# One decoder layer on one core: weights loaded in pairs, joined rows, a gate table laid out by tile

## The chip, the cores and the metric

One Trainium2 chip; the kernel runs on one of its cores. TensorE (PE in the profile) multiplies matrices, VectorE (DVE), ScalarE (ACT) and GpSimd (POOL) do elementwise work, SyncE (SP) issues transfers. The metric is device time in microseconds (us), lower is better.

## The reference

512 tokens of 1024 features go through one layer: a layer norm, two token mixers (a gated linear recurrence and pooled means), a second layer norm, and a mixer that looks up experts. This last part matters here. Each token picks 128 of 16384 experts (8 heads, 16 each) by its queries, with a gate for each:

```python
def peer_ffn(x, w_query, sub_keys, u_tab, v_tab):
    ...                                   # top 16 of each half, then of their sums
    expert = i1 * PEER_NKEYS + i2
    gate = jax.nn.softmax(best_v, axis=-1).astype(x.dtype)
    ...
        u = u_tab[et]
        act = jax.nn.gelu(jnp.einsum('td,tkd->tk', xt, u), approximate=False) * gt
        return jnp.einsum('tk,tkd->td', act, v_tab[et])
    ...
h = layer_norm(ALPHA * h + ffn + ple, ln2_g[l], ln2_b[l])
```

## The kernel before

The program has three stretches. In stage A (0 to about 445 us) PE works through the projections and the token mixers. In stage B (to about 924 us) the experts of all tokens are chosen. In stage C (to the end) the expert values are summed.

The experts are handled in two ways. The first 128 tokens (NG = 1 block) fetch the table rows they picked: an indirect transfer, issued by POOL in `issue`, brings one row of `u_tab` for each token (128x1024, 512 KB), and `consume` lets DVE multiply it with the token and sum (L984, the dot). After 128 of those one Gelu is taken of all the dots, and 128 rows of `v_tab` follow, which DVE adds with their gate (L987, the add). Two fetched rows share one buffer of 8 KB for each partition, of which there are four (`big`, pool `vt`); the layer norm's gain and bias (`gb`, from `gain_bias`) keep one of them from the start of stage C.

The other 384 tokens (ND) go over all 16384 experts densely, in NT = 128 tiles of 128 experts. For a tile `key_product` multiplies a tile of `u_tab` (128x1024) with the tokens on PE (24 matmuls `fp`), ACT takes the Gelu (`ge`, L633), `weigh` lets DVE multiply by the gates of this tile (`ge<-ge,gt`, L1009), `split_act` splits the product into two parts (ACT writes `ah`, DVE `al`; both L118/L119), and `values` multiplies them with a tile of `v_tab` and sums over all tiles in PSUM (18 matmuls `yacc`). Every matmul is done as three (L123 to L125) of split operands. So a weight tile (`wraw`) is also split, by `fetch`: ACT writes `wh` (L219) and DVE `wl` (L220), up to two tiles ahead of their use. The three `wraw` buffers hold 512 KB each.

The products of 52 tiles (NS) are made in stage B already and kept in DRAM (`Hs`), from where SP loads them back (`ge<-Hs`). `order` is the order of the tiles in stage C: eight tiles, and then stored and unstored ones in alternation. I call an iteration of the loop over tiles a U iteration if it also makes a key product, for the tile LEAD = 6 places later (70 of the 128), and a V iteration if not (58).

The gates of the dense tokens are built in stage B: PE makes them for 16 tokens at a time (`pG`), ACT copies them to `stg`, and SP writes 1 MB (`Gd<-stg`) to a DRAM table `Gd`, 24 times. In stage C `g_load` brings the gates for eight tiles at once (`gt<-Gd`, 1.5 MB, 16 times). In `Gd` the gates of 16 tokens and all experts stand together, so that such a load takes 24 pieces of 512 bytes for each partition. It is issued with the tile seven places ahead (`key_load`); three buffers hold gate tiles, and one more (`g0p`) the first.

The order of instructions on each engine in stages B and C is the order of the program text (`manual_schedule`), so each queue is in order: whatever waits holds all behind it on its engine. SP's queue holds nearly all loads. An iteration i of the loop before:

```python
key_load(i + LEAD + 1)
split_act(i + 1)
key_product(i + LEAD)
vals[i] = take()            # fetch: loads and splits weight tiles ahead
...                         # values(i, b), then consume() and issue()
weigh(i + LEAD)
```

Of the kernel before, what the change touches and what calls it, by code (L numbers as in the profile page):

```python
# [18 lines left out]
D = 1024  # L19
# [26 lines left out]
GEB = 9  # L46
W0 = ((1, 2), (3,), (), ())
PACE = (4, (1,))


@with_exitstack
def hybrid_block(ctx, tc, ins, out, dbg=None):
# [85 lines left out]

    def load_w(src):
        t = wp.tile([128, 1024], FT, name="wraw", tag="wraw", bufs=3)  # L140
        nc.sync.dma_start(t, src)
        return t
# [36 lines left out]
    order = list(range(NS, NS + VG))  # L179
    later = NT - NS - VG  # L180
    for i in range(NS + later):
        nf = (i + 1) * later // (NS + later)
        order.append(NS + VG + nf - 1 if nf > i * later // (NS + later) else i - nf)

    def u_src(e):
        return ins["u_tab_t"][e]

    def v_src(e):
        return ins["v_tab"][e * 128:(e + 1) * 128, :]

    act_hi, dve_hi, pool_lo, dve_lo = nc.scalar.copy, nc.vector.tensor_copy, nc.gpsimd.tensor_sub, nc.vector.tensor_sub
    stream, nu = [], 0
    for i in range(2 * H):
        stream.append((ins["w_query"][i], act_hi, pool_lo))
        for _ in range(UQ[i]):
            stream.append((u_src(nu), act_hi, pool_lo))
            nu += 1
    for q in range(4):
        stream += [(ins["w_ple_gate"][q, k], act_hi, pool_lo) for k in range(2)]
        for _ in range(UP[q]):  # L200
            stream.append((u_src(nu), act_hi, pool_lo))
            nu += 1
    stream += [(u_src(e), act_hi, dve_lo) for e in range(nu, NS)]
    for i in range(-LEAD, NT):
        if i + LEAD < NT and order[i + LEAD] >= NS:
            stream.append((u_src(order[i + LEAD]), act_hi, dve_lo))
        if i >= 0:
            stream.append((v_src(order[i]), act_hi, dve_lo))
    raws, parts, pos_ = {}, {}, [0, 0, 0]

    def fetch(n):
        while pos_[1] < min(n + 6, len(stream)) or pos_[2] < min(n + 3, len(stream)):
            if pos_[2] < min(n + 3, len(stream)) and pos_[1] - pos_[2] >= min(3, len(stream) - pos_[2]):
                i = pos_[2]
                _, f, g = stream[i]
# [3 lines left out]
                f(hi, raw)  # L219
                g(lo, raw, hi.bitcast(FT))  # L220
                parts[i] = (hi, lo)
                pos_[2] += 1
            else:
                raws[pos_[1]] = load_w(stream[pos_[1]][0])
                pos_[1] += 1
# [10 lines left out]
    with ExitStack() as pa:  # L236
        t2 = pa.enter_context(tc.tile_pool(name="t2", bufs=15))
# [235 lines left out]
        def att2(h):  # L473
            x = hd[h]
            v, hs = head(h)
            st = hp.tile([128, NB, DK], FT, name="st", bufs=2)
# [146 lines left out]
    Gd = dram.tile([ND // TG, 128, 128 * TG], FT, name="Gd")  # L623
# [41 lines left out]
    g0p = ctx.enter_context(tc.tile_pool(name="g0p", bufs=1))  # L665
# [10 lines left out]
    with ExitStack() as pb:  # L676
        rt = pb.enter_context(tc.tile_pool(name="rt", bufs=1))
        eqp = pb.enter_context(tc.tile_pool(name="eqp", bufs=3))
# [220 lines left out]
        def evacuate(s, p):  # L899
# [4 lines left out]
            if t4 == TG // 4 - 1:  # L904
                nc.sync.dma_start(Gd[g], stgs.pop(g).rearrange("p i t -> p (i t)"))
# [43 lines left out]
        g_load(order[0], g0p)  # L949
# [4 lines left out]
    with ExitStack() as pc:  # L954
# [5 lines left out]
        todo = [(0, b, k) for b in range(NG) for k in range(128)] + [(1, b, k) for b in range(NG) for k in range(128)]  # L960
        half_n = len(todo) // 2
        got, cnt, pair = {}, [0, 0], [None]

        def issue():
# [3 lines left out]
            kind, b, k = todo[n]  # L968
            if n % 2 == 0:
                pair[0] = big("rows").rearrange("p (a b) c -> p a (b c)", a=2)  # L970
            r = pair[0][:, n % 2, :]
            got[n] = r
            nc.gpsimd.indirect_dma_start(out=r, out_offset=None, in_=ins["v_tab" if kind else "u_tab"],  # L973
                                         in_offset=bass.IndirectOffsetOnAxis(ap=eidx[:, b, k:k + 1], axis=0))
            cnt[0] += 1

        def consume():
            n = cnt[1]
            if n >= len(todo) or n not in got:
                return  # L980
            kind, b, k = todo[n]
            r = got.pop(n)
            if kind == 0:
                nc.vector.scalar_tensor_tensor(r, r, 1.0, hg[:, b, :], op0=OP.mult, op1=OP.mult,  # L984
                                               accum_out=hdot[:, b, k:k + 1])
            else:
                nc.vector.scalar_tensor_tensor(hres[:, b, :], r, ggate[:, b, k:k + 1], hres[:, b, :],  # L987
                                               op0=OP.mult, op1=OP.add)
            cnt[1] += 1

        def key_load(i):
            if i < NT:
                g_load(order[i], gp)
# [22 lines left out]
        g2, b2 = gain_bias(2)  # L1016
# [34 lines left out]

        for i in range(LEAD + 1):
            key_load(i)
        for i in range(LEAD):
            key_product(i)
            weigh(i)
        split_act(0)
        GL = 4
        for _ in range(GL):
            issue()  # L1060
        share, tot = 0.0, sum(2 if e >= NS else 1 for e in order[:NT - TAIL - EARLY])
        budget = 0.0
        wait_n = 0
# [93 lines left out]
```

## Time and profile before

| | us |
|---|---|
| median of three runs | 1796.36 (1795.77 to 1797.86) |
| the profiled execution | 1800.53 |
| its span in the trace | 1798.8 |

The span is that of the trace's instructions; 1.7 us of the profiled execution lie around it. That execution is 4.2 us (0.23%) over the median. PE is busy in 97% of the span, DVE in 74%, ACT in 42%, POOL in 36%. An engine's busy time counts neither its waiting nor the issuing of transfers. "Wait" rows say which engine stood idle, ahead of which operation, and what ended it.

### The profile page before, as it was taken

The numbers are of one execution on the slowest core, as the hardware profiler recorded it, in microseconds if no ns is written. First come the engines' busy times: TensorE is split into PE (matmuls) and PEld (weight loads), VectorE is DVE, ScalarE is ACT, GpSimd is POOL, SyncE is SP. The second block draws the span as 40 slices with busy tenths as digits, with TensorE's granted clock in tenths as the row PEclk, the third lists the DMA queues.
The fourth block names the chain that finished last, engine by engine and source line by source line (L and its number), as shares of the span: only waits on it lengthen the run. The fifth ranks groups of instructions, "written<-read, shape, count | busy, mean of one in ns | idle before, by whom it ended". The sixth has DMA issues, their size and how long they took to land.

```text
span 1798.8 us, 25265 instructions
## 1 busy us (share of the span) xinstructions
PE 1750.0 (97%) x9677; PEld 1537.9 (85%) x9677; DVE 1327.0 (74%) x2332; ACT 749.4 (42%) x1052; POOL 644.5 (36%) x421
## 2 busy tenths in 40 slices
PE   7999999999999999999989999999999999999997
PEld 5888887888888998898989888888888888888886
DVE  6367764155589689999847797877867888878787
ACT  3578862332322445565643333333333333333332
POOL 3533333443355520000013453453433444445440
PEclk9999999999999999999999999999999999999999
DMA  4322222431333345565698999899998999899983
GB/s 147 117 83 71 71 74 93 127 123 60 108 105 107 97 138 183 192 229 202 236 303 291 350 344 366 314 331 331 315 331 295 338 352 343 301 342 338 320 303 104
DMA packets 159694, 399.10 MB, mean 222 GB/s; under 512 B 12882, under 2 KB 75858, under 8 KB 156372
## 3 DMA queue, kind: packets, MB, share of 16 engines
q1 hardware_dynamic: 115220, 253.02, 42.1%
q0 software_dynamic: 36864, 134.23, 20.9%
q10 hardware_dynamic: 7488, 10.23, 1.6%
q8 instruction: 76, 1.25, 0.3%
q14 instruction: 46, 0.38, 0.1%
HBM read 359.94 MB, written 37.49 MB: 221 GB/s over the span
## 4 chain that ended last, share of the span: by engine, by line
PE 82%; DVE 8%; DMA 6%; issue 2%; ACT 1%; SPq 0%; POOL 0%; ACTq 0%; DVEq 0%; POOLq 0%
PE fp L123 15%; PE fp L125 15%; PE fp L124 15%; PE yacc L124 8%; PE yacc L125 8%; PE yacc L123 8%; DMA wraw<-in_v_tab_dram 3%; PE ple L847 3%; PE pG L896 2%; DVE A L882 2%; DVE wl L220 2%; PE acc L124 1%; PE acc L125 1%; PE acc L123 1%; DVE oh L876 1%
## 5 line engine op out<-in xcount | busy, mean ns | idle before, releaser
L123 PE MATMUL fp<-othi,wh 128*128 128x384 f32 (+1 forms) x1216 | 430.1, 354 | 0.3 <-ACT othi L136 0.3
L125 PE MATMUL fp<-othi,wl 128*128 128x384 f32 (+1 forms) x1216 | 420.8, 346 | 5.5 <-DVE wl L220 5.5
L220 DVE TENSOR_TENSOR wl<-wraw,wh 128x1024 fp32r<-128x1024 f32 x246 | 300.9, 1226 | 163.1 <-ACT wh L219 161.3
L124 PE MATMUL fp<-otlo,wh 128*128 128x384 f32 (+1 forms) x1216 | 420.0, 345 | 0.2 <-DVE otlo L137 0.2
L219 ACT CAST wh<-wraw 128x1024 fp32r<-128x1024 f32 x280 | 294.3, 1053 | 300.5 <-DMA wraw<-in_v_tab_dram 192.6
L973 POOL DMA_INDIRECT rows<-in_u_tab_dram,eidx x128 | 178.6, 1395 | 499.7 <-DVE oh L876 249.3
L123 PE MATMUL yacc<-wh,ah 128*128 128x512 f32 x768 | 300.9, 392 | 6.2 <-ACT wh L219 6.2
L124 PE MATMUL yacc<-wl,ah 128*128 128x512 f32 x768 | 302.6, 394 | 3.6 <-DVE wl L220 3.6
L125 PE MATMUL yacc<-wh,al 128*128 128x512 f32 x768 | 301.9, 393 | 0.0
L973 POOL DMA_INDIRECT rows<-in_v_tab_dram,eidx x128 | 188.3, 1471 | 224.0 <-DVE hres L987 188.5
L119 POOL TENSOR_TENSOR wl<-wraw,wh 128x1024 fp32r<-128x1024 f32 x68 | 169.9, 2501 | 255.5 <-ACT wh L118 255.4
L125 PEld LDWEIGHTS fp<-othi,wl 128*128 128x128 f32 x1216 | 229.9, 189 | 13.4 <-DVE wl L220 5.9
L124 PEld LDWEIGHTS fp<-otlo,wh 128*128 128x128 f32 x1216 | 230.4, 189 | 10.3 <-DVE otlo L137 0.5
L123 PEld LDWEIGHTS fp<-othi,wh 128*128 128x128 f32 x1216 | 230.1, 189 | 10.2 <-ACT othi L136 0.5
L633 ACT ACTIVATE ge<-fp 128x384 f32<-128x384 f32 x128 | 62.9, 492 | 358.6 <-PE fp L125 357.2
L123 PEld LDWEIGHTS yacc<-wh,ah 128*128 128x128 f32 x768 | 145.1, 189 | 36.1 <-ACT wh L219 7.4
L124 PEld LDWEIGHTS yacc<-wl,ah 128*128 128x128 f32 x768 | 145.2, 189 | 35.4 <-DVE wl L220 6.4
L125 PEld LDWEIGHTS yacc<-wh,al 128*128 128x128 f32 x768 | 145.2, 189 | 30.7 <-DVE al L119 0.3
L987 DVE SCALAR_TENSOR_TENSOR hres<-rows,ggate,hres 128x1024 f32<-128x1024 f32 x128 | 164.2, 1283 | 2.4
L984 DVE SCALAR_TENSOR_TENSOR rows<-rows,hg 128x1024 f32<-128x1024 f32 x128 | 151.2, 1221 | 0.3 <-DMA rows<-in_u_tab_dram,eidx 0.3
L123 PE MATMUL fp<-xthi,wh 128*128 128x512 f32 x352 | 142.4, 405 | 0.3 <-DVE q L426 0.3
L125 PE MATMUL fp<-xthi,wl 128*128 128x512 f32 x352 | 137.3, 390 | 0.0
(245 smaller groups left out, 2462.0 us busy)
## 6 DMA issues: line engine op xcount, KB each, us to landing
wraw<-in_u_tab_t_dram SPq DMA_DIRECT2D x128, 512.0 KB
wraw<-in_v_tab_dram SPq DMA_DIRECT2D x128, 512.0 KB
Gd<-stg SPq DMA_DIRECT2D x24, 1024.0 KB
gt<-Gd SPq DMA_DIRECT2D x16, 1536.0 KB
wraw<-in_w_in_dram SPq DMA_DIRECT2D x44, 512.0 KB
Hs<-ge ACTq DMA_DIRECT2D x52, 192.0 KB
ge<-Hs SPq DMA_DIRECT2D x52, 192.0 KB
wraw<-in_w_query_dram SPq DMA_DIRECT2D x16, 512.0 KB
```

Source lines behind the costliest of these rows:

```text
L119: lo_eng.tensor_sub(lo, src, hi.bitcast(FT))
L123: nc.tensor.matmul(o, a[0], b[0], start=start, stop=False)
L124: nc.tensor.matmul(o, a[0], b[1], start=False, stop=False)
L125: nc.tensor.matmul(o, a[1], b[0], start=False, stop=stop)
L219: f(hi, raw)
L220: g(lo, raw, hi.bitcast(FT))
L633: nc.scalar.activation(ge, p[:, :ND], AF.Gelu)
L847: nc.tensor.matmul(o, a[x], b[y], start=(cc == 0 and blk % 2 == 0 and n == 0), stop=(cc == NCK - 1 and n == 2), skip_group_check=True)
L882: nc.vector.tensor_tensor(x, oh[:, :OG // 2], gT[:, j, t * OG:(t + 1) * OG] .rearrange("p (u v) -> p u v", v=2)[:, :, None, :] .to_broadca ...
L973: nc.gpsimd.indirect_dma_start(out=r, out_offset=None, in_=ins["v_tab" if kind else "u_tab"], in_offset=bass.IndirectOffsetOnAxis(ap=eidx[ ...
L984: nc.vector.scalar_tensor_tensor(r, r, 1.0, hg[:, b, :], op0=OP.mult, op1=OP.mult, accum_out=hdot[:, b, k:k + 1])
L987: nc.vector.scalar_tensor_tensor(hres[:, b, :], r, ggate[:, b, k:k + 1], hres[:, b, :], op0=OP.mult, op1=OP.add)
```

## The change

1. **Weights in pairs.** The tiles of the weight stream lie in DRAM in the order of use, two to a row of 8 KB for each partition. One load brings 1 MB, into one of two `wraw` buffers of 128x2048, once no more than two loaded tiles are unsplit.
2. **Joint rows.** `u_tab` and `v_tab` lie side by side (8 KB a row). 128 indirect loads of 128x2048 (1 MB) take the place of 256 of 512 KB. `consume(n)` does the dot of row n on DVE, a Gelu and a multiplication of one column on ACT (128x1, 256 such in all), and the add of row n−1. The two passes and the Gelu between them are gone. A row keeps its buffer until its add, and two rows are on order ahead of use.
3. **Gate table by tile.** `Gd` holds the gates of eight tiles together: a gate load reads 12 KB in one piece for each partition. The 24 writes `Gd<-stg` are cut in 512-byte pieces instead (16 for each partition).
4. **Gate products later.** `weigh` stands two tiles ahead of use (WLEAD), not six, and `g_load` four tiles ahead, behind `weigh`. There are three gate buffers in all. The first gate load comes after the first key product of stage C, and the first row gathers in stage C, not before it.
5. **The last norm's gain and bias** are loaded at iteration 6. Some buffers are cut to make room: `ge` from 9 to 8, temporaries of stage A and of the choice of experts by one.

The diff's core:

```diff
+WLEAD = 2
-GEB = 9
+GEB = 8
...
     def fetch(n):
+        while pos_[2] < min(n + 3, len(stream)) or (pos_[1] < len(stream) and pos_[1] - pos_[2] <= 2):
+            if pos_[1] < len(stream) and pos_[1] - pos_[2] <= 2:
+                t = wp.tile([128, 2048], FT, name="wraw", tag="wraw", bufs=2)
+                nc.sync.dma_start(t, ins["wstream"][pos_[1] // 2])
+                raws[pos_[1]], raws[pos_[1] + 1] = t[:, :1024], t[:, 1024:]
+                pos_[1] += 2
...
-    Gd = dram.tile([ND // TG, 128, 128 * TG], FT, name="Gd")
+    Gd = dram.tile([NT // VG, 128, ND // TG, VG * TG], FT, name="Gd")
...
-            nc.sync.dma_start(gt, Gd[:, :, j * VG * TG:(j + 1) * VG * TG].rearrange("g p x -> p g x"))
+            nc.sync.dma_start(gt, Gd[j])
...
-                nc.sync.dma_start(Gd[g], stgs.pop(g).rearrange("p i t -> p (i t)"))
+                nc.sync.dma_start(Gd[:, :, g, :].rearrange("j p x -> p j x"),
+                                  stgs.pop(g).rearrange("p (j i) t -> p j (i t)", i=VG))
...
+            got[n] = big("rows").rearrange("p a b -> p (a b)")
+            nc.gpsimd.indirect_dma_start(out=got[n], out_offset=None, in_=ins["uv_tab"],
...
+            nc.vector.scalar_tensor_tensor(r, r, 1.0, hg[:, b, :], op0=OP.mult, op1=OP.mult, accum_out=hd)
+            nc.scalar.activation(hd, hd, AF.Gelu)
+            nc.scalar.mul(hd, hd, ggate[:, b, k:k + 1])
+            if n:
+                add_value(n - 1)
...
-            weigh(i + LEAD)
+            weigh(i + WLEAD)
+            if i + WLEAD + 2 < NT:
+                g_load(order[i + WLEAD + 2], gp)
+            if i == LEAD:
+                g2, b2 = gain_bias(2)
```

The order on PE is the same in both kernels, and on DVE, ACT and POOL it is the same through stages A and B. Three places of stage C follow; what stands in brackets is what a row waits for.

DVE in the loop before, a V iteration from one `weigh` to the next (L984 is the dot, L1009 `weigh`):

```order
L1009 TENSOR_TENSOR ge<-ge,gt 128x384
L119 TENSOR_TENSOR al<-ge,ah 128x384 [waits Activation_49]
L220 TENSOR_TENSOR wl<-wraw,wh 128x1024 [waits DMAHW2_49,PE_49,Activation_49]
L984 SCALAR_TENSOR_TENSOR rows,hdot<-rows,hg 128x1024 [waits DMASW2_49,DVE_49]
L984 SCALAR_TENSOR_TENSOR rows,hdot<-rows,hg 128x1024 [waits DMASW3_49]
L984 SCALAR_TENSOR_TENSOR rows,hdot<-rows,hg 128x1024 [waits DMASW4_49,DVE_49]
L1009 TENSOR_TENSOR ge<-ge,gt 128x384 [waits DMAHW3_49]
```

and now, a U iteration from its `weigh` on (L1019 is `weigh`, L993 the dot, L984 the add):

```order
L1019 TENSOR_TENSOR ge<-ge,gt 128x384
L151 TENSOR_TENSOR al<-ge,ah 128x384 [waits Activation_49]
L233 TENSOR_TENSOR wl<-wraw,wh 128x1024 [waits DMAHW3_49,Activation_49]
L233 TENSOR_TENSOR wl<-wraw,wh 128x1024 [waits PE_49,Activation_49]
L993 SCALAR_TENSOR_TENSOR rows,hdot<-rows,hg 128x1024 [waits DMASW6_49]
L984 SCALAR_TENSOR_TENSOR hres<-rows,hdot,hres 128x1024
```

Where there were dots alone, each dot now has an add of the row before behind it, ahead of the next `weigh`.

ACT in the loop before (L118 writes `ah`, L219 `wh`):

```order
L633 ACTIVATE ge<-fp 128x384 [waits PE_49]
L219 CAST wh<-wraw 128x1024 [waits DMAHW0_49,DVE_49]
L118 CAST ah<-ge 128x384
L219 CAST wh<-wraw 128x1024 [waits DMAHW1_49,DVE_49]
L118 CAST ah<-ge 128x384 [waits DMAHW2_49]
L219 CAST wh<-wraw 128x1024 [waits DMAHW3_49,DVE_49,PE_49]
```

and now (L150 writes `ah`, L232 `wh`, L994 and L995 are the two small operations of `consume`):

```order
L643 ACTIVATE ge<-fp 128x384 [waits PE_49]
L232 CAST wh<-wraw 128x1024 [waits DMAHW7_49]
L994 ACTIVATE hdot<-hdot 128x1 [waits DVE_49]
L995 ACTIVATE hdot<-hdot,ggate 128x1 [waits Activation_49]
L150 CAST ah<-ge 128x384 [waits DVE_49]
L232 CAST wh<-wraw 128x1024
```

`ah` waited for no other engine before, since its `weigh` had been done five iterations earlier; now it waits for the `weigh` that DVE has just been given. The small operations wait for the dot.

SP at the start of stage C before (L672 loads gates, L96 the gain and bias, L141 weights):

```order
L905 DMA Gd<-stg 128x2048 [waits DMAHW0_49,Activation_49]
L672 DMA gt<-Gd 128x24x128 [waits DMAHW2_49,DMAHW5_49,DMAHW0_49,PE_49]
L96 DMA gb<-in_ln_g_dram 128x1024 [waits DMAHW3_49,PE_49]
L96 DMA gb<-in_ln_b_dram 128x1024 [waits DMAHW4_49]
L672 DMA gt<-Gd 128x24x128 [waits PE_49]
L141 DMA wraw<-in_u_tab_t_dram 128x1024 [waits DMAHW6_49,DVE_49]
```

and now (L914, L681 and L224 for the same three kinds):

```order
L224 DMA wraw<-in_wstream_dram 128x2048 [waits DMAHW7_49,DVE_49]
L914 DMA Gd<-stg 128x16x128 [waits DMAHW0_49,Activation_49]
L681 DMA gt<-Gd 128x3072 [waits DMAHW2_49,DMAHW4_49,DMAHW1_49,DMAHW5_49,DMAHW0_49,PE_49]
L224 DMA wraw<-in_wstream_dram 128x2048 [waits DMAHW3_49,DVE_49]
L224 DMA wraw<-in_wstream_dram 128x2048 [waits DMAHW7_49,DMAHW4_49,DVE_49]
```

One gate load stands ahead of the first weights of stage C, where there were two and the norm's vectors.

## Rows read from the trace of the kernel before

**Rows 1.** The page's first part: busy time of each engine, share of the span, instructions
```profile
PE 1750.0 (97%) x9677; PEld 1537.9 (85%) x9677; DVE 1327.0 (74%) x2332; ACT 749.4 (42%) x1052; POOL 644.5 (36%) x421
```

**Rows 2.** The waits: us in total, times, longest
```profile
ACT ge L633 <- PE fp L125: 357.2, 118, 6.2
...
DVE ge L1009 <- DMA gt<-Gd: 28.2, 5, 13.3
```

**Rows 3.** Windows: busy us, instructions, granted clock, DMA share, GB/s
```profile
720.00:820.00 100.00, 94.31 (x800) 86.75 (x799) 93.69 (x117) 58.37 (x71) 0.00 (x0) 0.97 0.59 209
925.00:940.00 15.00, 9.45 (x54) 9.13 (x53) 2.05 (x3) 3.35 (x5) 1.88 (x2) 0.89 1.09 353
940.00:960.00 20.00, 20.00 (x104) 19.61 (x104) 9.33 (x13) 7.97 (x13) 0.00 (x0) 0.91 0.74 230
980.00:1000.00 20.00, 20.00 (x96) 17.37 (x95) 18.71 (x29) 7.44 (x11) 10.66 (x9) 1.00 1.00 386
1100.00:1200.00 100.00, 100.00 (x491) 88.95 (x490) 78.84 (x119) 34.58 (x49) 46.80 (x32) 1.00 0.92 322
1200.00:1400.00 200.00, 193.99 (x919) 169.96 (x918) 151.52 (x212) 65.57 (x92) 81.04 (x60) 0.97 0.94 323
1500.00:1700.00 200.00, 196.38 (x954) 173.09 (x953) 160.53 (x168) 68.57 (x96) 93.90 (x62) 1.00 0.93 325
```

**Rows 4.** The chain that ended last, around 920: start, us, what
```profile
920.29 5.23 DMA Gd<-stg
925.59 12.28 DMA gt<-Gd
```

**Rows 5.** SyncE's queue around 1200: start, us, what
```profile
1193.19 0.43 SPq L672 DMA_DIRECT2D gt<-Gd  x1
1193.67 8.37 SPq L996 DMA_DIRECT2D ge<-Hs  x1
...
1206.34 10.61 SPq L141 DMA_DIRECT2D wraw<-in_v_tab_dram  x1
```

**Rows 6.** ScalarE's timeline; in brackets the idle time before and its releaser
```profile
1107.18 0.49 ACT L633 ACTIVATE ge<-fp 128x384 f32<-128x384 f32 x1 [3.16 <-PE fp L125]
1107.57 1.04 ACT L219 CAST wh<-wraw 128x1024 fp32r<-128x1024 f32 x1
1108.51 0.51 ACT L118 CAST ah<-ge 128x384 fp32r<-128x384 f32 x1
1108.92 1.05 ACT L219 CAST wh<-wraw 128x1024 fp32r<-128x1024 f32 x1
1115.49 0.49 ACT L633 ACTIVATE ge<-fp 128x384 f32<-128x384 f32 x1 [5.51 <-PE fp L125]
...
1127.88 0.49 ACT L633 ACTIVATE ge<-fp 128x384 f32<-128x384 f32 x1 [3.46 <-PE fp L125]
...
1224.09 1.04 ACT L219 CAST wh<-wraw 128x1024 fp32r<-128x1024 f32 x1 [10.62 <-DMA wraw<-in_v_tab_dram]
```

**Rows 7.** VectorE's timeline at three places
```profile
1108.64 1.23 DVE L220 TENSOR_TENSOR wl<-wraw,wh 128x1024 fp32r<-128x1024 f32 x1 [2.30 <-ACT wh L219]
1109.79 1.22 DVE L984 SCALAR_TENSOR_TENSOR rows<-rows,hg 128x1024 f32<-128x1024 f32 x1
...
1222.13 0.56 DVE L1009 TENSOR_TENSOR ge<-ge,gt 128x384 f32<-128x384 f32 x1 [4.38 <-DMA gt<-Gd]
...
1413.75 1.28 DVE L987 SCALAR_TENSOR_TENSOR hres<-rows,ggate,hres 128x1024 f32<-128x1024 f32 x1
1414.95 0.55 DVE L1009 TENSOR_TENSOR ge<-ge,gt 128x384 f32<-128x384 f32 x1
```

**Rows 8.** GpSimd's timeline: one row gather
```profile
979.62 1.30 POOL L973 DMA_INDIRECT rows<-in_u_tab_dram,eidx  x1 [0.30 <-issue]
```

**Rows 9.** VectorE's timeline: the use of that gather
```profile
988.39 1.27 DVE L984 SCALAR_TENSOR_TENSOR rows<-rows,hg 128x1024 f32<-128x1024 f32 x1 [0.26 <-DMA rows<-in_u_tab_dram,eidx]
```

**Rows 10.** The instructions of line 271: duration ns min/median/max, first and last start
```profile
L271 ACT ACTIVATE mv<-mv,eps x4: 290/296/298, 5.2 to 28.6; 128x1 f32<-128x1 f32 x4
```

More of the change, by code (lines that the diff above doesn't have):

```diff
@@ L45, with tile_order, weight_stream @@
 LEAD = 6
-GEB = 9
+WLEAD = 2
+GEB = 8
 W0 = ((1, 2), (3,), (), ())
 PACE = (4, (1,))
+def tile_order():
+    order = list(range(NS, NS + VG))
+    later = NT - NS - VG
+    for i in range(NS + later):
+        nf = (i + 1) * later // (NS + later)
+        order.append(NS + VG + nf - 1 if nf > i * later // (NS + later) else i - nf)
+    return order
+def weight_stream():
+    order, stream, nu = tile_order(), [], 0
+    for i in range(2 * H):
+        stream.append(("query", i))
+        stream += [("u", nu + k) for k in range(UQ[i])]
+        nu += UQ[i]
+    for q in range(4):
+        stream += [("ple", 2 * q + k) for k in range(2)]
+        stream += [("u", nu + k) for k in range(UP[q])]
+        nu += UP[q]
+    split_at = len(stream)
+    stream += [("u", e) for e in range(nu, NS)]
+    for i in range(-LEAD, NT):
+        if i + LEAD < NT and order[i + LEAD] >= NS:
+            stream.append(("u", order[i + LEAD]))
+        if i >= 0:
+            stream.append(("v", order[i]))
+    return stream, split_at
 @with_exitstack
@@ L176, in tok_half @@
             emit(half, blk, accs[blk])
[L179 to L208, printed above, removed]
+    order = tile_order()
+    stream, split_at = weight_stream()
     raws, parts, pos_ = {}, {}, [0, 0, 0]
     def fetch(n):
-        while pos_[1] < min(n + 6, len(stream)) or pos_[2] < min(n + 3, len(stream)):
-            if pos_[2] < min(n + 3, len(stream)) and pos_[1] - pos_[2] >= min(3, len(stream) - pos_[2]):
+        while pos_[2] < min(n + 3, len(stream)) or (pos_[1] < len(stream) and pos_[1] - pos_[2] <= 2):
[4 more added lines that the diff above has]
+                pos_[1] += 2
+            else:
                 i = pos_[2]
-                _, f, g = stream[i]
                 hi = wp.tile([128, 1024], FR, name="wh", tag="wh")
@@ L475, in att2 @@
             v, hs = head(h)
[L476 removed]
+            st = hp.tile([128, NB, DK], FT, name="st", bufs=1)
             pd = bank("pd")
@@ L958, in hybrid_block @@
         gs, acts, vals = {}, {}, {}
-        todo = [(0, b, k) for b in range(NG) for k in range(128)] + [(1, b, k) for b in range(NG) for k in range(128)]
-        half_n = len(todo) // 2
-        got, cnt, pair = {}, [0, 0], [None]
+        todo = [(b, k) for b in range(NG) for k in range(128)]
+        got, cnt = {}, [0, 0]
         def issue():
@@ L1114, in lay_out @@
     w_in = a["w_in"][0]
+    tiles = {
+        "query": feat(a["w_query"][0]),
+        "ple": a["w_ple_gate"][0].reshape(2, 4, 128, 4, 256).transpose(3, 0, 2, 1, 4).reshape(8, 128, 1024),
+        "u": a["u_tab"][0].reshape(128, 128, 8, 128).transpose(0, 3, 2, 1).reshape(128, 128, 1024),
+        "v": a["v_tab"][0].reshape(128, 128, 1024),
+    }
+    w = np.stack([tiles[name][i] for name, i in weight_stream()[0]])
     return {
```

71 lines of the change are left out of this document (28 added, 43 removed).

## The prediction

> **What bounds the kernel now.** I read the page's first part first. PE is busy for 97% of the span and DVE for 74% [rows 1], so PE is the bound, and its order and matmuls are untouched. Only what keeps PE from working can be won, and PE loses time in few places. The waits come next: ACT waits 357.2 us for PE ahead of `ge` [rows 2]. That is the sound state of the loop, where ACT and DVE are early and PE sets the pace. The pace itself is seen on ACT between one `ge` and the next: 8.31 us from 1107.18 to 1115.49, a U iteration alone, and 12.39 us from there to 1127.88, a U and a V iteration [rows 6]. So V takes 4.08 us.
>
> Then I read the windows for stretches that fall off this pace [rows 3]. 1100 to 1200 is undisturbed, with PE at 100 us of 100 and 491 matmuls, so a matmul is worth 100/491 = 0.204 us there. Twice that is 982 for 200 us; the two stretches that are not of this kind have 919 (1200 to 1400) and 954 (1500 to 1700). They lose 63 × 0.204 = 12.8 us and 28 × 0.204 = 5.7 us. A matmul count takes in the lower clock that follows a stall (0.97 granted in the first). At the start of stage C, PE is idle for 15.00 − 9.45 = 5.5 us from 925 to 940, and the granted clock is 0.91 in the 20 us after it, which is 1.8 us more. Together stage C loses 5.5 + 1.8 + 12.8 + 5.7 = 25.8 us.
>
> What ends these stalls is one thing. The chain that ended last runs through a gate load, 12.28 us from 925.59 [rows 4]. DVE waits for `gt` five times, 28.2 us in all [rows 2], one of them at 1222.13 [rows 7]. SP does worse than wait for it: in SP's queue the row behind a gate load takes 8.37 us at 1193.67, and the next one behind such a load 10.61 us at 1206.34 [rows 5], when a transfer is otherwise handed over in some 0.4 us, as `gt` itself is (0.43 us). Meanwhile no weights are loaded: at 1224.09 ACT had been idle for 10.62 us until `wraw` came [rows 6], and PE ran dry.
>
> **The gate table and its loads: −25.8 us.** A gate load was 24 pieces of 512 bytes for each of 128 partitions, 3072 in all; it becomes one run of 12 KB for each. I read the blocked SP as the cost of so many pieces in one queue. This can be set beside a row on the 16 transfer engines: 925 to 940, with gates and the norm's vectors under way, shows a DMA share of 1.09 at 353 GB/s, and 980 to 1000, with larger pieces, 1.00 at 386 GB/s [rows 3]. So small pieces cost 386/(353/1.09) = 1.19 times the engine time; the larger cost is the queue behind. I take all of the 25.8 us as removed, the upper bound, because gates, weights and the stored `ge` share SP's queue in every one of these places; the lower bound is nothing, if the stall has a cause other than the pieces.
>
> The Trainium skill speaks against this: its page "DMA: Bandwidth & Descriptors", section "Specifications", gives 512 bytes as the smallest transfer that runs at the full rate. By that a gate load in 512-byte pieces would gain nothing from longer ones, the 25.8 us would stay, and the change would end up slower by its other terms. The 1.19 above disagrees mildly and the row of 8.37 us strongly.
>
> **The gate table's writes: +1 us.** 24 writes of 1 MB now carry 2048 pieces of 512 bytes each, and they stand in the same queue as stage B's weights. By the factor 1.19 each takes 0.19 × 5.23 us [rows 4] = 1.0 us longer. Stage B is covered: from 720 to 820 the DMA share is 0.59, and what PE lacks there (94.31 us of 100) is due to DVE, busy for 93.69 us [rows 3]. Nothing waits for a write until the first gate load. If the cover goes, SP is held by each write as it was by each gate load. Ends: 0 and 24 us (1.0 us for each write); taken 1, for the last one, which is on the path at 920.29.
>
> **The start of stage C: within the 25.8.** Before, the first two gate loads and the gain and bias stood ahead of the first weights in SP's queue. Now one gate load does, and it begins to be needed only when the key products ahead of it are made; in exchange the first row gathers start a few us later, and DVE has no dots to do yet. I cost both at nothing. The gain and bias at iteration 6 take a buffer that rows would have, and are counted with the rows below.
>
> **The loop of ACT and DVE: 0 by itself, its spare 12 us.** Before, an `ah` found its product weighed long ago. Now `ah` waits for the `weigh` that stands at the end of DVE's work, and `wl`, at the beginning of that work, waits for the `wh` behind `ah`. So the two engines run in a ring, once around in each iteration. In a V iteration with one row: `weigh` 0.55 [rows 7], `ah` 0.41 (1108.51 to 1108.92), `wh` 1.05 [rows 6], `wl` 1.15, dot 1.15 by `wl`'s cadence for the same size, add 1.20 (1413.75 to 1414.95) [rows 7], and two handovers of 0.03 (`wh` ends at 1108.61, `wl` starts at 1108.64), 5.57 us. In a U iteration ACT has `ge` (0.39) and a second `wh` (0.94) in addition [rows 6], 6.90 us. Set against PE: U 6.90 against 8.31, V 5.57 against 4.08, a pair 12.47 against 12.39. Where U and V alternate the ring and PE are level, and over all 128 iterations the ring takes 70 × 6.90 + 58 × 5.57 = 806 us and PE 70 × 8.31 + 58 × 4.08 = 818 us. It costs nothing if nothing else waits in it, but whatever does wait in it is seen by PE. The two small operations cost about 0.29 us each (128x1) [rows 10] and run on ACT while DVE adds (1.20) and weighs (0.55); they are hidden, as the work on ACT behind them waits for `weigh` anyway. Without that cover, 128 × 0.6 = 77 us.
>
> **The joint rows in this ring: +12 us.** The dots and adds themselves are as many as before. What is new is the time allowed to a gather. Row n+2 is ordered when the add of row n−1 has set its buffer free, and its dot comes two rows later. With one row in each iteration this allows, from the start of the add, 5.57 + 6.90 − 1.15 = 11.3 us. In the changed order 22 iterations hold two rows; 17 of them follow an iteration that has a row too, and there the third row must be in after one iteration: 6.90 + 2.35 − 1.15 = 8.1 us for 12 of them (U), and 5.57 + 1.20 = 6.8 us for 5 (V). What a gather needs: the add 1.20, some 0.3 until POOL starts, and then the landing. For the landing of 1 MB the trace of before has two bounds. From below: POOL's own 1.30 us [rows 8] and 5.23 us for 1 MB that SP wrote [rows 4], 6.5 us. From above: the 512 KB gather of 979.62 was only in at 988.39 [rows 8, 9], 8.8 us with its neighbours under way. I take 7.0, nearer to the lower end because only two gathers can be out at once now. So 8.5 us are needed, and the 12 wait 0.4 each and the 5 wait 1.7: 4.8 + 8.5 = 13.3 us. About 1 us of it goes into PE's reserve of split weights: 12. At the lower end (8.0 needed) it is 5 × 1.2 = 6 us, at the upper end (10.3) 12 × 2.2 + 5 × 3.5 = 44 us.
>
> **Weights in pairs, fewer gate buffers: +2 us.** A pair is set free only by the `wl` of its second half, and with two buffers the next pair must land while the other is being split: two tiles, about 10 us, against 5.23 us for a transfer of this size [rows 4]. A gate tile's buffer is freed by its last `weigh`, about two iterations (12 us) before the next tile of the same kind is due, and SP holds at that load until then, with weights behind it. 1.5 MB at the rate of the 5.23 us is 7.8 us. Both fit, with no great margin in a stretch whose DMA share is 0.92 [rows 3]. Ends 0 and 15 us (one us for each of the 15 gate loads behind the first); taken 2.
>
> **Sum.** 1800.5 − 25.8 + 1 + 12 + 2 = 1789.7 for the profiled execution, which was 0.23% over the median: 1786 us.
>
> **Rivals.**
> *The ring and the gathers take more than the gates gave (slower).* The place is `ah` waiting for `weigh` while DVE's dot in front of it waits for `rows`. It decides from the point where a landing takes more than about 8.2 us: then 9.7 are needed, 12 × 1.6 + 5 × 2.9 = 34 us in place of 13, less the reserve. At 8.8 it is 44, that is 1800.5 − 25.8 + 44 + 3 = 1822, or 1818 by the median; at 8.2, 1807. For it: the gather of 988.39, the level ring, and a DMA share of 0.92. Against it: half as many pieces for the same bytes of rows, and transfers that come with fewer of their kind at once.
> *The stalls move but stay (no change).* A gate load of 1.5 MB still lies in front of weights, now issued four tiles ahead instead of seven. If half of the 25.8 us comes back, with 12 for the rows and 3 for the rest: 1803, 1798 by the median. For it: a gate load that DVE must free a buffer for holds SP as long as before. Against it: the SP rows of 8 to 11 us are the hand-over behind it, not a buffer.
> *Nearly all is won.* Gathers land in 6.5 us or are covered by slack that I don't count, and the whole 25.8 us stays won: 1800.5 − 25.8 + 0 to 6 = 1775 to 1781, 1771 to 1777 by the median. For it: the ring has 12 us to spare over the loop. Against it: that spare lies in U iterations and can't be saved up for later.
>
> **How the numbers follow.** The forecast with its own range, 1777 to 1792, has a chance of 0.36; nearly all won 0.18; no change, about 1793 to 1800, 0.18; slower 0.28. What a measurement of this kernel can tell from no change is about 0.2%, 3.6 us; so faster 0.54, same 0.18, slower 0.28. For 8 in 10 the range reaches from 1772, near the end of the full gain, to 1807, where the slower rival's landing is 8.2 us.
>
> **What the profile after would show.** Right: no SP row of 8 us behind a gate load; no wait of `ge` for `gt` above 2 us; PE without idle time at 925 to 940 and 491 matmuls in each undisturbed 100 us; waits of the dot for `rows` of some 13 us in total, at iterations of two rows; `ah` waiting for `weigh` in most iterations. Wrong: DVE waiting for `rows` in most iterations, or ACT waiting for `wraw` as long as before, or PE waiting for `wl` regularly in V iterations. The prediction would be wrong above all if a gather of 1 MB lands much later than 7 us, or if the writes hold SP in stage B.

## The result, and the profile after

The changed kernel takes 1814.56 us (median of four runs, 1811.58 to 1816.51); the ratio to the kernel before, measured beside it, is 1.0095 with a 95% interval of 1.0075 to 1.0115. Forecast were 1786 us and a range to 1807. So it became slower, by 0.95%, and the rival on that side was right in its place (ACT's `ah` waiting for `weigh`), but its condition, late rows alone, was only part of it. The profiled execution took 1816.51 us, its span is 1814.8 us.

The page's first part for the changed kernel, as in [rows 1]:

```profile
PE 1757.4 (97%) x9677; PEld 1538.2 (85%) x9677; DVE 1343.2 (74%) x2331; ACT 810.3 (45%) x1307; POOL 417.2 (23%) x293
```

PE is still busy for 97%, by an average that tells nothing. The waits, which answer to [rows 2]:

```profile
ACT ah L150 <- DVE ge L1019: 157.2, 123, 3.4
ACT ge L643 <- PE fp L157: 117.7, 62, 4.4
...
DVE rows L993 <- DMA rows<-in_uv_tab_dram,eidx: 16.9, 11, 4.5
...
ACT wh L232 <- DMA wraw<-in_wstream_dram: 10.9, 5, 3.6
...
DVE ge L1019 <- DMA gt<-Gd: 2.3, 2, 1.4
```

The gate wait is gone (28.2 us before, 2.3 now). But `ge`, where ACT waits for PE, has fallen from 357.2 to 117.7 us, and `ah` waits for `weigh` for 157.2 us, 123 times. Taken for the loop alone, 1000 to 1700:

```profile
ACT ah L150 <- DVE ge L1019: 129.4, 104, 2.6
...
ACT ge L643 <- PE fp L157: 1.1, 1, 1.1
```

In 700 us of the loop ACT waited for PE once. ACT and DVE are no longer early there; they are level with PE at best (1400 to 1500, below). One turn of them, from one `weigh` (L1019) to the next in a V iteration, on both engines' timelines:

```profile
995.86 0.55 DVE L1019 TENSOR_TENSOR ge<-ge,gt 128x384 f32<-128x384 f32 x1
...
996.45 0.51 ACT L150 CAST ah<-ge 128x384 fp32r<-128x384 f32 x1 [1.14 <-DVE ge L1019]
...
996.87 1.05 ACT L232 CAST wh<-wraw 128x1024 fp32r<-128x1024 f32 x1
...
997.95 1.23 DVE L233 TENSOR_TENSOR wl<-wraw,wh 128x1024 fp32r<-128x1024 f32 x1 [0.40 <-ACT wh L232]
...
999.09 1.22 DVE L993 SCALAR_TENSOR_TENSOR rows<-rows,hg 128x1024 f32<-128x1024 f32 x1
...
1000.24 1.28 DVE L984 SCALAR_TENSOR_TENSOR hres<-rows,hdot,hres 128x1024 f32<-128x1024 f32 x1
...
1001.43 0.55 DVE L1019 TENSOR_TENSOR ge<-ge,gt 128x384 f32<-128x384 f32 x1
```

995.86 to 1001.43 is 5.57 us, the sum that the prediction made from rows of before, and nothing in it is idle beyond the hand-overs: `weigh`, `ah`, `wh`, `wl`, dot, add, `weigh`. U iterations with one row take 6.89 us in the same way (6.90 predicted), iterations with two rows 7.91 and 9.23 us.

The windows, which answer to [rows 3]:

```profile
925.00:940.00 15.00, 15.00 (x89) 15.00 (x88) 4.91 (x4) 5.16 (x7) 1.03 (x2) 1.00 0.86 305
...
1100.00:1200.00 100.00, 95.81 (x459) 82.79 (x458) 78.40 (x97) 39.44 (x75) 14.76 (x14) 1.00 0.86 326
...
1400.00:1500.00 100.00, 100.00 (x491) 88.97 (x491) 82.97 (x105) 41.14 (x80) 17.45 (x16) 1.00 0.89 335
1500.00:1700.00 200.00, 195.67 (x938) 171.87 (x937) 162.18 (x202) 82.01 (x156) 34.67 (x31) 0.98 0.88 324
```

925 to 940 is won: PE is busy all the time at a granted clock of 1.00, the 2.4 GHz level throughout (before 9.45 of 15 us, at a mean of 0.89 after the idle time). From 1400 to 1500 the loop is at full pace with 491 matmuls. But 1100 to 1200 has 459 where before it had 491; 1500 to 1700 has 938 where before it had 954.

SyncE's queue behind the gate loads, the row of `ge<-Hs` and then that of the weights (ns min/median/max):

```profile
L1006 SPq DMA_DIRECT2D ge<-Hs x52: 326/427/1010, 956.6 to 1737.5; - x52
```

```profile
L224 SPq DMA_DIRECT2D wraw<-in_wstream_dram x140: 327/328/385, 424.3 to 1771.8; - x140
```

The longest hand-over of weights is 0.39 us and of `ge` 1.01 us, against 10.61 and 8.37 us in [rows 5]. So the blocked queue is gone as predicted, and the loss is new. One of the stops of PE, on the timelines of several engines:

```profile
1046.28 0.33 SPq L681 DMA_DIRECT2D gt<-Gd  x1
...
1054.04 0.56 DVE L1019 TENSOR_TENSOR ge<-ge,gt 128x384 f32<-128x384 f32 x1 [1.36 <-DMA gt<-Gd]
...
1054.63 0.51 ACT L150 CAST ah<-ge 128x384 fp32r<-128x384 f32 x1 [2.59 <-DVE ge L1019]
...
1058.70 1.04 ACT L232 CAST wh<-wraw 128x1024 fp32r<-128x1024 f32 x1 [3.56 <-DMA wraw<-in_wstream_dram]
...
1059.79 0.49 PE L155 MATMUL yacc<-wh,ah 128*128 128x512 f32 x1 [1.16 <-ACT wh L232]
```

A gate load is issued at 1046.28. The `weigh` that needs a gate tile waits 1.36 us for it, the weights behind it come 3.56 us late for `wh`, and PE stops at once (1.16 us, and again for `wl`). Another kind of lateness:

```profile
1603.91 0.33 SPq L681 DMA_DIRECT2D gt<-Gd  x1
...
1614.76 1.23 DVE L993 SCALAR_TENSOR_TENSOR rows<-rows,hg 128x1024 f32<-128x1024 f32 x1 [4.45 <-DMA rows<-in_uv_tab_dram,eidx]
...
1619.21 0.79 PE L155 MATMUL yacc<-wh,ah 128*128 128x512 f32 x1 [3.04 <-ACT wh L232]
```

Again a gate load goes out (1603.91); the dot at 1614.76 had waited 4.45 us for its row, and PE stops for 3.04 us. In the kernel before, the stop at 1224.09 came when ACT had waited for 10.62 us [rows 6]; here 3.56 us and a 1.36 before it do it.

At the end there is a stop with no transfer in it:

```profile
1778.61 1.28 DVE L1035 BATCH_NORM_STATS2 st<-hres 128x6 f32<-128x512 f32 x2
...
1784.63 0.55 DVE L1019 TENSOR_TENSOR ge<-ge,gt 128x384 f32<-128x384 f32 x1
1785.21 0.51 ACT L150 CAST ah<-ge 128x384 fp32r<-128x384 f32 x1 [3.39 <-DVE ge L1019]
...
1785.78 0.80 PE L155 MATMUL yacc<-wh,ah 128*128 128x512 f32 x1 [1.64 <-ACT ah L150]
```

The weighing of one of the last four tiles (1784.63) stands on DVE behind the norm of the first token block (from 1778.61), which in the kernel before came after the last `weigh`:

```profile
1762.71 0.56 DVE L1009 TENSOR_TENSOR ge<-ge,gt 128x384 f32<-128x384 f32 x1
...
1766.46 1.28 DVE L1026 BATCH_NORM_STATS2 st<-hres 128x6 f32<-128x512 f32 x2
```

Now ACT waits 3.39 us for `weigh` and PE 1.64 us for `ah`, and a second time in the same way. The last `ge<-fp` starts at 1769.08 in a span of 1814.8 us, 45.7 us before the end; in the kernel before it was 38.7 us (1760.10 in 1798.8). So 7.0 of the 16.0 us between the two spans arise behind the last `ge`.

### The profile page after: what moved, and what is told of

Same layout as the page of the kernel before. It is cut to its first block, busy times and chain, and to the rows that moved or that the text cites. A ratio compares the mean times of both kernels' runs of the same rounds, so it can differ in the third digit from the quotient of the medians.

```text
span 1814.8 us, 24732 instructions
## 1 busy us (share of the span) xinstructions
PE 1757.4 (97%) x9677; PEld 1538.2 (85%) x9677; DVE 1343.2 (74%) x2331; ACT 810.3 (45%) x1307; POOL 417.2 (23%) x293
## 4 chain that ended last, share of the span: by engine, by line
PE 42%; issue 39%; DVE 8%; POOL 7%; DMA 2%; ACT 1%; SPq 0%; POOLq 0%; ACTq 0%; DVEq 0%
PE fp L155 10%; PE fp L157 9%; PE fp L156 9%; POOL rows L978 7%; PE ple L856 3%; PE pG L905 2%; DVE A L891 2%; PE acc L156 1%; PE acc L157 1%; PE acc L155 1%; DVE wl L233 1%; DVE oh L885 1%; DMA rows<-in_uv_tab_dram,eidx 1%; PE sc L800 1%; DVE eq L753 1%
## 5 line engine op out<-in xcount | busy, mean ns | idle before, releaser
L978 POOL DMA_INDIRECT rows<-in_uv_tab_dram,eidx x128 | 139.7, 1091 | 955.4 <-DVE hres L984 672.4
L232 ACT CAST wh<-wraw 128x1024 fp32r<-128x1024 f32 x280 | 293.3, 1049 | 17.4 <-DMA wraw<-in_wstream_dram 10.9
L156 PEld LDWEIGHTS yacc<-wl,ah 128*128 128x128 f32 x768 | 146.0, 190 | 40.8 <-DVE wl L233 11.9
L993 DVE SCALAR_TENSOR_TENSOR rows<-rows,hg 128x1024 f32<-128x1024 f32 x128 | 156.1, 1219 | 17.0 <-DMA rows<-in_uv_tab_dram,eidx 16.9
L994 ACT ACTIVATE hdot<-hdot 128x1 f32<-128x1 f32 x128 | 26.0, 203 | 316.3 <-DVE rows L993 316.3
L984 DVE SCALAR_TENSOR_TENSOR hres<-rows,hdot,hres 128x1024 f32<-128x1024 f32 x128 | 163.9, 1281 | 0.1
L156 PE MATMUL fp<-xtlo,wh 128*128 128x512 f32 x352 | 137.2, 390 | 0.0
```

Source lines behind the costliest of these rows:

```text
L156: nc.tensor.matmul(o, a[0], b[1], start=False, stop=False)
L232: nc.scalar.copy(hi, raw)
L978: nc.gpsimd.indirect_dma_start(out=got[n], out_offset=None, in_=ins["uv_tab"], in_offset=bass.IndirectOffsetOnAxis(ap=eidx[:, b, k:k + 1], ...
L984: nc.vector.scalar_tensor_tensor(hres[:, b, :], got.pop(n)[:, D:], hdot[:, b, k:k + 1], hres[:, b, :], op0=OP.mult, op1=OP.add)
```

## The experiments

Each ratio is to runs of the kernel before on the same chip, whose medians lay between 1795.9 and 1799.9 us; where two experiments are close, compare ratios. Behind a ratio stands its 95% interval.

**e1: weigh four tiles ahead.**

```diff
-WLEAD = 2
+WLEAD = 4
```

> The changed kernel with weigh four tiles ahead of use in place of two (gate loads stay two ahead of weigh, so they move with it). Theory ring (ACT's ah waits for the weigh that DVE has just been given, so that ACT and DVE go round in a ring as long as PE's pace, and each late transfer becomes PE time): the wait of ah for weigh, 157 us, goes nearly to 0, the idle stretches of PE in the loop and the 4 us in the tail go, 1780 to 1792 us. Theory gathers (two joint rows ahead are too few, whatever ACT waits for): the waits of the dot for rows, 17 us, stay and most of the loss stays, 1805 to 1815 us.

1784.8 us, ratio 0.9936 (0.9920 to 0.9953): 30 us faster than the changed kernel by the medians, with one number changed (it moves the gate loads two iterations earlier too; e9 and e13 take that apart). The waits:

```profile
ACT ge L643 <- PE fp L157: 210.1, 109, 4.2
...
DVE rows L993 <- DMA rows<-in_uv_tab_dram,eidx: 28.5, 17, 4.3
...
ACT wh L232 <- DMA wraw<-in_wstream_dram: 16.2, 11, 4.3
...
DVE ge L1019 <- DMA gt<-Gd: 14.8, 3, 7.5
```

The wait of `ah` for `weigh` is not in the list any more, and ACT waits for PE again (210.1 us). Yet rows (28.5 against 16.9 us), weights (16.2 against 10.9) and gates (14.8 against 2.3) all come later for those who use them, presumably because these ask sooner. The windows from 1000 to 1700, of the changed kernel and of e1:

```profile
1000.00:1700.00 700.00, 683.23 (x3279) 598.82 (x3278) 564.87 (x702) 286.01 (x546) 118.16 (x108) 0.99 0.87 327
...
1000.00:1700.00 700.00, 696.87 (x3396) 617.32 (x3395) 563.64 (x721) 288.77 (x561) 119.91 (x112) 1.00 0.90 340
```

3396 matmuls in place of 3279, where the full pace of [rows 3] would give 7 × 491 = 3437. The theory of the ring holds; that of the gathers falls as the main cause, since more waiting for rows goes with less loss.

**e2: no gathers after the first two.** `issue` gives back one of two rows:

```diff
+            if n >= 2:
+                got[n] = keep[n % 2]
+                cnt[0] += 1
+                return
```

> The changed kernel with only the first two row gathers; all dots and adds are done, on these two rows again and again (the other rows are left out, and the dot writes to a buffer of its own). Theory gathers: without late rows and their traffic the loss is gone, 1780 to 1790 us. Theory ring: the ring's own 6.89 and 5.57 us remain and iterations of two rows still stop PE, but no landing is late, so part of the loss stays: 1790 to 1800 us, and ah still waits for weigh in most iterations.

1789.4 us, 0.9964 (0.9951 to 0.9976). The waits:

```profile
ACT ah L150 <- DVE ge L1024: 156.3, 124, 3.4
...
ACT wh L232 <- DMA wraw<-in_wstream_dram: 2.8, 2, 1.4
```

The ring stands, as closed as before (156.3 us), with only 2.8 us of late weights and 0.2 us of late gates in it, and 25 us are won. From 1000 to 1700:

```profile
ACT ge L643 <- PE fp L157: 2.1, 2, 1.1
```

ACT hardly ever waits for PE here either, as in the changed kernel, though PE keeps its pace (below). So that missing wait shows a ring without slack, and not yet a loss: the loss in the loop needs late transfers besides.

**e6: ring open and no gathers.** Both edits.

> Ring open and gathers gone at once (the rows after the first two are left out): the fourth corner beside the changed kernel (1814.6), ring open alone (1784.8) and gathers gone alone (1789.4). If the two losses were independent, 30 and 25 us would add up and it would be 1760 us. If late landings cost only because the ring has no slack (one loss seen from two sides), little is left to win: 1774 to 1782 us.

1776.9 us, 0.9890 (0.9865 to 0.9915). This is the fourth corner:

| | gathers | no gathers | gathers cost |
|---|---|---|---|
| ring closed (two ahead) | 1814.6 | 1789.4 | 25.2 |
| ring open (four ahead) | 1784.8 | 1776.9 | 7.9 |
| the ring costs | 29.8 | 12.5 | |

The table goes by medians from several chips. By the ratios the gathers cost 23.5 and 8.3 us and the ring 28.6 and 13.3; the part that only the two together cost is 15 us, give or take 7 by the intervals.

The windows from 1000 to 1700, of e2 and of e6:

```profile
1000.00:1700.00 700.00, 697.94 (x3400) 617.84 (x3399) 583.49 (x725) 296.77 (x566) 0.00 (x0) 1.00 0.47 170
...
1000.00:1700.00 700.00, 700.00 (x3418) 621.79 (x3418) 564.68 (x727) 291.27 (x567) 0.00 (x0) 1.00 0.47 170
```

In e6 PE does not stop. A matmul is worth 0.204 us, so against its 3418 the changed kernel's 3279 are 28 us, e2's 3400 are 3.7 and e1's 3396 are 4.5 (estimates by count). In the same 700 us the waits for rows, weights and gates sum up to 26.1 us in the changed kernel (16.5, 7.3 and 2.3), 3.0 in e2 and 43.1 in e1 (26.8, 9.0 and 7.3). With the ring closed PE loses about what comes late; with it open, a tenth of it.

The ring costs 12.5 us with no gather late, and most of this is the tail: from the last `ge` to the end e2 takes 46.5 us and e6 39.3, 7.2 us less. The lateness of the gathers, and of what shares the transfer engines with them, costs 7.9 us by itself; but 17 us more arise where ring and lateness meet.

**e4: the ring alone, put into the kernel before.** `weigh(i + LEAD)` becomes `weigh(i + 2)`, with the gate load of tile i + 4 behind it.

> The kernel before with weigh two tiles ahead and the gate loads four ahead behind it, alone (single rows in two passes, old gate table, single weights). Theory ring: the ring is there with single rows too, so the stalls of before stay and late landings cost more, 1805 to 1825 us. Theory gathers: nothing of the joint rows is in it, so it is as before but for the first loads, 1790 to 1800 us.

1840.9 us, 1.0258 (1.0240 to 1.0275): 45 us slower, more than I expected at most. The waits:

```profile
ACT ah L118 <- DVE ge L1008: 532.2, 124, 7.8
```

Here V iterations have up to three dots in a row between `wl` and `weigh`, as on DVE and then ACT at 1106.52:

```profile
1106.52 1.23 DVE L220 TENSOR_TENSOR wl<-wraw,wh 128x1024 fp32r<-128x1024 f32 x1 [0.39 <-ACT wh L219]
...
1111.10 0.55 DVE L1008 TENSOR_TENSOR ge<-ge,gt 128x384 f32<-128x384 f32 x1
...
1111.68 0.51 ACT L118 CAST ah<-ge 128x384 fp32r<-128x384 f32 x1 [5.20 <-DVE ge L1008]
```

`ah` had to wait 5.20 us for three dots; the ring is longer than PE's 4.08 by far. Nothing of the joint rows is needed for the loss. Nor do the later gate loads explain it: DVE waited for gates for 22.1 us in all, and for 28.2 before.

**e3: the gate table alone, put into the kernel before.** Only the layout of `Gd`, its reads and writes.

> The kernel before with the gate table laid out by tile alone. If the 512-byte pieces of the gate loads were the cause of the stalls of before (my 25.8 us), SP's rows of 8 us behind a gate load go to 0.4 us and the time falls to 1771 to 1778 us. Rival: the 1.5 MB themselves, not their pieces, hold the weights up: half or more of the stalls stay, 1785 to 1797 us.

1780.2 us, 0.9919 (0.9902 to 0.9935), 15.8 us faster. The row of `ge<-Hs` in SP's queue, before and in e3, and e3's window from 1000 to 1700:

```profile
L996 SPq DMA_DIRECT2D ge<-Hs x52: 422/427/8719, 961.7 to 1734.7; - x52
...
L997 SPq DMA_DIRECT2D ge<-Hs x52: 420/426/1598, 957.8 to 1714.2; - x52
...
1000.00:1700.00 700.00, 700.00 (x3416) 621.39 (x3415) 568.38 (x721) 243.17 (x342) 325.57 (x225) 1.00 0.93 340
```

The longest is 1.6 us, 8.7 before, and PE doesn't stop in the loop. The old layout was the cause of the blocked queue. That it was the number of its pieces, and not the spacing of their addresses in DRAM, which changed with it, is my reading; no run separates the two. 25.8 us were too many to expect of it (below).

**e7: the old gate table, with the ring open.**

> Ring open (weigh four ahead), all of the change but the gate table, which keeps its old layout (24 pieces of 512 bytes for each partition). If the new table is worth inside the changed kernel what it was worth alone (15.8 us): 1797 to 1804 us, with SP's rows of some 8 us behind a gate load back. If paired weights and joint rows had made the old table harmless: 1784 to 1790 us.

1801.5 us, 1.0023 (1.0010 to 1.0036), 16.7 us over e1. SP's queue at one place:

```profile
1220.40 0.38 SPq L681 DMA_DIRECT2D gt<-Gd  x1
1220.83 10.26 SPq L1005 DMA_DIRECT2D ge<-Hs  x1
```

The blocked queue is back. The table is worth the same in either kernel (15.8 and 16.7 us).

**e5: rows spread evenly, ring closed**, and **e11: the same with the ring open.**

```diff
-            budget += len(todo) * (2 if order[i] >= NS else 1) / tot
+            budget += 1 + 1 / 16
```

> The changed kernel, ring and all (weigh two ahead), with one row in nearly every iteration in place of 0, 1 or 2 (17 rows in 16 iterations). Theory doubles (the loss in the ring comes from iterations of two rows, where the ring takes 9.2 or 7.9 us and the next gather has the short time): the idle stretches at those iterations go, waits of the dot for rows fall from 17 us to under 8, 1795 to 1804 us. Theory level ring (6.89 + 5.57 = 12.46 against PE's 12.39 leaves nothing to catch up with, so any late landing costs, wherever the rows stand): gates and weights still come late now and then, 1806 to 1815 us.

> Ring open (weigh four ahead) and rows spread evenly. With the ring closed the even rows made it no better (1819.8 for 1814.6). With it open, ACT and DVE have time in hand in U iterations, and the two-row iterations with their short times for a gather are gone: 1776 to 1782 us. If spreading gives nothing: 1783 to 1788 us, as with the ring open alone.

e5: 1819.8 us, 1.0134 (1.0108 to 1.0160); e11: 1785.3 us, 0.9927 (0.9902 to 0.9953). Both times the even spread gives nothing. In e5 the dot still waited 16.0 us for rows, 16 times, and `wh` 19.4 us for weights. My idea that the iterations with two rows were at fault falls; that a ring level with PE loses by any lateness, wherever the rows stand, fits. Nor does the spread help an open ring.

**e9: weigh two ahead, but in front of the dots.** `weigh(i + WLEAD)` moves ahead of the loop over `consume` and `issue`.

> The changed kernel, weigh still two tiles ahead, but standing in front of the iteration's dots and adds on DVE, not behind them; the gate loads stay where they are. Theory ring: ah then waits only for a weigh behind wl, the ring is shorter by dot and add (2.35 us for each row), and the loss goes as with weigh four ahead: 1781 to 1790 us. Rival: what helped with four ahead was that the gate loads moved two iterations earlier with it; then the loss stays, 1805 to 1815 us.

1795.6 us, 0.9988 (0.9971 to 1.0005): 19 of the 30 us. The waits:

```profile
ACT ah L150 <- DVE ge L1019: 36.0, 19, 3.4
...
DVE ge L1019 <- DMA gt<-Gd: 12.6, 7, 3.6
```

The order on DVE is most of it. Of the 11 us that e9 lacks against e1, 5.7 lie in the tail: from the last `ge<-fp` to the end it takes 46.5 us and e1 40.8, since `weigh` two ahead still comes behind the norm there. What is left in the loop are fewer waits of the same kind (19 of `ah`, 36.0 us over the whole span): `weigh` is now ahead of its `ah` by the dots and adds of one iteration and by no more, and where it waits for gates itself (12.6 us), `ah` does too.

**e13: weigh four ahead, gate loads one tile ahead of weigh in place of two**, and **e14: weigh four ahead and in front of the dots**, to see whether the rest was late gates or the order:

> Weigh four ahead, gate loads one tile ahead of weigh in place of two, so that a gate load has one iteration less to land. If late gates are what the weigh put in front of the dots still paid (the 11 us between 1795.6 and 1784.8): DVE waits for gt longer than the 15 us of weigh four ahead, 1792 to 1800 us. If an open ring takes late gates in its slack: 1784 to 1788 us.

> Weigh four ahead and in front of the dots and adds. If the order in front of the dots costs something of its own (DVE then waits for gates with dots still to do): 1788 to 1797 us. If it was late gates only: as with four ahead, 1782 to 1787 us.

e13: 1788.0 us, 0.9943 (0.9917 to 0.9968); e14: 1787.1 us, 0.9927 (0.9901 to 0.9953). Neither can be told from e1 (0.9936). In e13 DVE waits 26.7 us for gates, more than in any other run with the new table, and it costs nothing that can be measured: with two more iterations between `weigh` and `ah` such a wait has room. So what e9 lacked in the loop, some 5 us, is not late gates by themselves, and not the order. That it is the little room left in e9 fits both runs, but is argued and not shown. In the tail e13 and e14 take 39.4 and 39.3 us.

**e10: the add in front of the dot**, weigh two ahead (the label's "wlead4" is a slip).

> The changed kernel with the add of row n-1 in front of the dot of row n, so that the next gather is ordered 1.15 us earlier; weigh two ahead as in the changed kernel, so the ring is closed. Theory level ring: late rows fall by some 10 us in sum, of which a part comes back: 1800 to 1810 us. If gate loads and weights set the loss: 1810 to 1816 us.

1813.2 us in a single run, so no interval; against 1814.6 it settles nothing more than that there is no large gain. Its trace says why there need be none: the dot's waits for rows fall from 16.9 to 1.0 us, but the add, now close behind the small operations of the dot before it, waits for ACT 22 times, 13.1 us in all. So one wait in the ring may stand in for another.

**e8: the table with the later start** (first gate load behind the first key product, norm vectors at iteration 6) in the kernel before.

> The kernel before with the gate table by tile, and from the change also the later first gate load (behind the first key product, four gate buffers in one pool) and the norm's vectors at iteration 6; single rows, single weights and weigh six ahead stay. The start of stage C was won by 7.5 us in the changed kernel and by 3.8 with the table alone, so this should give some 4 us on the 1780.2 of the table alone: 1774 to 1778 us. If the start was won by the pairs instead: 1780 us again.

1780.5 us, 0.9905 (0.9881 to 0.9929), as e3. The start of stage C:

```profile
925.00:940.00 15.00, 10.55 (x58) 10.23 (x58) 2.94 (x4) 4.28 (x6) 2.51 (x3) 0.97 1.00 390
```

It is no better than with the table alone: PE is busy for 10.55 of 15 us, in e3 for 11.72. Two gate loads still go out together here, at 926.25, ahead of most of the weights. In e12 (below), as in the changed kernel, the second comes 23 us behind the first, the weights come in pairs, and PE is busy for all 15 us. So the later start alone does not win the start, and whether the pairs or the second gate load do is not shown.

**e12: single rows in the changed kernel, ring open.** `issue` and `consume` of before, two passes, the rest as in e1.

> Ring open (weigh four ahead), gate table by tile, weights in pairs, first gate load and norm vectors as in the changed kernel, but single rows of the two tables in two passes as in the kernel before (no small operations on ACT, four rows on order). Beside the ring opened alone (1784.8) it shows what the joint rows cost with the ring open, beside the table alone (1780.2) what the pairs and the later start are worth. Theory joint rows cost (28.5 us of waits for rows, some 8 us by the run without gathers): 1774 to 1780 us, the fastest of all. If the joint rows cost nothing once the ring is open: 1783 to 1787 us.

1778.2 us, 0.9898 (0.9870 to 0.9926): the fastest kernel that computes all, beside 0.9919 of the table alone, from which its interval does not part it. Against e1 the joint rows cost 6.6 us (0.9936 to 0.9898; the intervals overlap a little). The waits:

```profile
ACT ge L643 <- PE fp L157: 396.3, 116, 8.5
...
ACT wh L232 <- DMA wraw<-in_wstream_dram: 223.6, 58, 10.7
```

ACT has no small operations in the loop and waits for weights instead, and PE is waited for longest (396.3 us), as in the kernel before.

## Why the prediction was wrong

**Gate table, −25.8 us: mechanism right, size wrong.** It measured −15.8 alone (e3) and −16.7 in the changed kernel with the ring open (e7 to e1). I had taken the upper bound, the whole loss of stage C against a loop that never stops. The loop's part is won in full: in e3 PE is busy for all of 1000 to 1700. But of the start of C the table alone wins only a part (PE busy for 11.72 of 15 us from 925 to 940, 9.45 before), and the 25.8 were read from one execution that took 4.2 us over the median: the two profiled executions, 1800.53 and 1780.05, differ by 20.5 us, the medians by 15.8. The Trainium skill's rule from "DMA: Bandwidth & Descriptors", section "Specifications" (512 bytes run at full rate), would have had nothing to win here. The queue's row went from 8.7 us to 1.6 with longer pieces, so the trace did not agree with what I made of the rule.

**Writes, +1 us: not refuted.** No write held SP. Their price is seen in the windows: from 700 to 800 the changed kernel moved 214 GB/s at a DMA share of 0.71, the one before 212 GB/s at 0.61, a factor 1.15 over all traffic, and nothing waited for it. From its first `ge` in stage B (492.25 us before, 493.47 now) to its last (921.36 and 923.88) the changed kernel took 1.3 us longer than the kernel before; the other kernels with the new writes stand between −1.0 and +1.3 there.

**The start of C: right in what came of it.** 5.5 us of idle time and the 0.91 clock are gone. Which part of the change did it is open (e8).

**"The loop of ACT and DVE: 0 by itself, its spare 12 us": this is the step that failed.** The periods were right to 0.01 us, and I saw that U and V pairs were level (12.47 against 12.39). I then set the sum over the loop against PE's sum, 806 against 818, and called the difference spare, against my own remark that it lies in U iterations and can't be saved up. The ring has no queue between its parts, so a late transfer in it makes it late for good, and level pairs never win it back: the 26.1 us of late transfers from 1000 to 1700 and the 28 us of PE's loss there. I had also said that whatever waits in the ring is seen by PE, but charged only the rows for it; weights and gates, late by 10.9 and 2.3 us over the span, stood in the sum with 2. With no gather late the ring cost 12.5 us, not 0, 7.2 of them in the tail, which I had left out altogether: that `weigh` now comes behind the norm was a step of the change that I didn't follow to the last tiles. With gathers it cost 29.8, some 5 in the tail (45.7 us after the last `ge` against 40.8 in e1) and 25 in the loop.

**Joint rows, +12 us.** Waits of the dot for rows: 16.9 us against the 13.3 predicted. That the sums are near is partly luck: predicted were 17 waits of 0.4 and 1.7 us at iterations of two rows, measured 11, of up to 4.45 us, four of them at iterations of one row. And it is not the dot's waits alone that count. With the ring open they are longer (28.5 us) and the joint rows cost 6.6 us (e1 against e12); with the ring closed all gathers cost 25.2.

**Pairs and gate buffers, +2 us: right with the ring open, not with it closed.** e12 has pairs and late start and is no slower than e3. In the changed kernel late weights and gates make 13.2 us of waits in the ring, near the upper end of 15 that I gave. No run has single weights in the closed ring, so what the pairs do to this is not known.

Put together by the medians: −15.8 (table) − 2.0 (pairs and start) + 6.6 (joint rows) + 29.8 (ring) = 18.6 us, and the changed kernel is 17.5 over the kernel before beside it. These steps lead from one measured kernel to the next, so they must add up, and the 1.1 us left over are the difference between two medians of the kernel before; the sum confirms nothing. It is one path through the corners; the ring's part would be 12.5 to 29.8 depending on what else is late. The rival that I gave 0.28 named the right wait, but decided by a landing of 8.2 us, which was the wrong variable: any lateness in the ring did it, of weights and gates as of rows.

What stays open: which part of the 7.9 us of gathers in an open ring is late rows and which is their traffic in the way of weights and gates. No run here separates them.

## What to carry to other kernels

Where a change makes one in-order engine wait for another's last instruction, and that other one waits for the first one's next, add up the ring and set it against the bound's period for each iteration, not over the loop: if it is level, price it as a loss, since late transfers now reach the bound nearly in full. Moving a producer closer to its use saves buffers and spends the room that hid lateness; two iterations more of that room were worth 30 us here. Before taking a stall as removed in full, ask which of its places the edit reaches and whether the execution that it was read from is a typical one, and look at the tail, where an early instruction's new place can be behind something it never met before.

## What was not expected of the hardware

A load of 3072 pieces of 512 bytes held up the next transfer in SP's queue by 8 to 11 us [rows 5], while a write of 2048 such pieces in the changed kernel did not: the longest `wraw` hand-over behind these was 0.39 us. The two differ in the number of pieces, in direction and in the spacing of addresses, and no run here tells which it is.
